# Order of the vector work in a seven-product channel mixer: the fourth sum's two halves moved up, the second sum put behind the first ones

## The chip, the cores and the metric

The kernel runs on one core of a Trainium2 chip. A core has five engines with instruction queues of their own: TensorE (PE, matrix products; its weight loads are shown apart as PEld), VectorE (DVE, elementwise work), ScalarE (ACT, activations, copies and casts), GpSimd (POOL) and SyncE (SP), which here only issues transfers. The engines meet through semaphores alone: an instruction waits in its queue until what it reads has been written and what it overwrites has been read, and everything behind it in the same queue waits too.

The metric is the device time of one launch in microseconds. A difference of about 0.2% (2.7 us) is what a measurement of this kernel can tell from no change.

## The reference

The reference is a two-layer encoder trunk for 512 positions of width 1024, in float32. Each layer has a mixer (layer 0 a recurrent time mixer, layer 1 chunked attention, each beside attention into 256 memory tokens) and then a channel mixer. The change lies in the channel mixer, which is the same in both layers:

```python
def conv_glu(h, w_in, conv_w, conv_b, w_out):
    seq = h.shape[1]
    gate, val = jnp.split(h @ w_in, 2, axis=-1)
    gp = jnp.pad(gate, ((0, 0), (CONV_W - 1, 0), (0, 0)))
    conv = conv_b + sum(conv_w[j] * gp[:, j:j + seq] for j in range(CONV_W))
    return (jax.nn.gelu(conv, approximate=False) * val) @ w_out
```

The hidden width is 2816, that is 22 tiles of 128 gate columns and 128 value columns; the convolution has three taps along the positions. What the mixer returns is added to the residual stream.

## The kernel before

Activations lie transposed in on-chip memory: 128 features on the partitions, 512 positions along the row. Products keep float32 accuracy by splitting both factors into a rounded high half and the rest as a low half, and adding high x high, high x low and low x high. For weights the cast to the high half is done by ACT (`high`, L468) and the subtraction that leaves the low half by DVE (`lower`, L473).

Of the 22 hidden tiles of a layer, tiles 0 to 5 and 21 are computed plainly (`plain`). Tiles 6 to 20 go "by seven": the product of gate and value weights with the activations is cut into 2 x 2 blocks (gate or value columns; first or second half of the input features; first or second half of the positions), and seven block products of sums and differences replace the eight that the plain way needs (the scheme of Strassen and Winograd). Each of these 15 tiles has one call of `Seven.frame`; one call is a frame below. In the profile, layer 0 has its 15 frames from 456 to 611 us and layer 1 from 1033 to 1188 us.

The raw weights of a tile lie in one buffer `raw` with seven slots of 128x512: gate half one (G1), gate half two (G2), value half one (V1), value half two (V2), and the sums S2, S3, S1. The slot of V1 later takes the fourth sum S4. There are two such buffers, so tile j+1 uses the one that tile j-1 has left. Three transfers fill it, issued by SP at L441 (G2 and V2, 512 KB) and L443 (V1, then G1, 256 KB each), as soon as the last reader of the old tile is through.

The sums are DVE's:
- the first ones, `sums` (L455): S3 = G1 + V1 and S1 = V2 + V1 in one instruction of 128x1024;
- the second, `sum2` (L460): S2 = S1 + G1;
- the fourth, `sum4` (L464): S4 = S2 + G2, written where V1 stood.

The casts on ACT then work on neighbouring slots: `high(G1)` casts G1 and S2 together, so it comes after `sum2`.

PE does the seven products of a frame (`prod`, L420 for the two with the weights' high half, L422 for the one with the low half), each with 8 + 4 matmuls of 256 columns, into four accumulators f1 to f4: G1 into f1 (first half), S2 into f2, S3 into f1 (second half), S1 into f3, V2 into f3, G2 into f4, S4 into f4 (second half). A product's low-half matmuls come after its eight high-half ones.

DVE's queue in one frame, before, is in this order (the letters in brackets are used below; "previous" and "next" are the neighbouring tiles):
- [end1] previous tile: add f4 to the gate, L478
- [w31] low half of S3 and S1 of this tile, L473, 128x1024
- [taps] two convolution steps of the previous tile, L485 and L486
- [g] L517, reads f2
- [sums] of the next tile, L455
- [c] L526, reads f1
- [sum2] of the next tile, L460
- [w4] low half of S4 of this tile, L473, 128x512: the last reader of this tile's `raw`
- [end5] previous tile: gate times value, L492
- [gs] low half of G1 and S2 of the next tile, L473, 128x1024
- [sum4] of the next tile, L464
- [v] L537 and [g2] L539, read f3

ACT's queue in one frame: cast of G2 and V2 (L468), copy of f1 (L509), the convolution's first tap for the previous tile (`end2`, L481), the cast of S4 (L468, 128x512), the previous tile's Gelu (`end4`, L489), a negated copy of G2 and V2 of the next tile (`rest`, L450), the cast of G1 and S2 of the next tile, the cast of S3 and S1 of the next tile. Behind `rest`, POOL issues a transfer (L451, 512 KB) that adds the weights once more onto that negated high half, which leaves their low half; this tile of weights is `wlv`.

These instructions are marked to keep the order of the program (`keep`) on their engine. What is not marked, the plain tiles and the splits for the output projection, is put between by a planner.

Of the kernel before, what the change touches and what calls it, by code (L numbers as in the profile page):

```python
# [19 lines left out]
S = 512  # L20
# [92 lines left out]
def trunk_kernel(ctx, tc, A, out):  # L113
# [37 lines left out]
    def ps_f():  # L151
        return banks["F"].tile([P, S], F32, name="psf", tag="psf")
# [8 lines left out]
    def tmp(dt=F32, shape=(P, S)):  # L161
        return banks["tmp"].tile(list(shape), dt, name="tmp", tag="tmp")
# [214 lines left out]
    def ffn(l, hp, U, M, N, new_u, xT, after, last=None):  # L377
# [38 lines left out]
        def prod(ps, w, x):  # L416
            (wh, wl), o = w
            for k in range(4):
                for n in range(2):
                    PE.matmul(ps, wh[:, o + k * P:o + k * P + P], x[k][n], start=k == n == 0, stop=False)  # L420
            for k in range(4):
                PE.matmul(ps, wl[:, o + k * P:o + k * P + P], x[k][0], start=False, stop=k == 3)  # L422
# [3 lines left out]
        def keep(ins):  # L426
            return tc.keep_in_program_order(ins) if pinned[0] else ins
# [3 lines left out]
        S4 = V1  # L431

        class Seven:
# [68 lines left out]
            def frame(self, prev, nxt):  # L502
                if nxt:
                    nxt.load()
                f1, f2, f3, self.f4 = (ps_f() for _ in range(4))
                g, c, v = self.g, self.c, self.v = tmp(), tmp(), tmp()
                prod(f1[:, h1], (self.gs, 0), XN(0, 0))
                hv = self.high(G2)
                keep(SC.copy(g[:, h1], f1[:, h1]))  # L509
                if prev:  # L510
                    prev.end1()
                    prev.end2()
                w31 = self.lower(S3, self.h31)
                if prev:
                    prev.end3()
                prod(f2[:, h1], (self.gs, S), XT(T2))
                keep(V.tensor_tensor(g[:, h2], g[:, h1], f2[:, h1], op=ALU.subtract))  # L517
                h4 = self.high(S4, S)
                if nxt:
                    nxt.sums()  # L520
                if prev:
                    prev.end4()
                if nxt:
                    nxt.rest()
                prod(f1[:, h2], (w31, 0), XT(T3))
                keep(V.tensor_tensor(c[:, h1], f1[:, h2], g[:, h2], op=ALU.subtract))  # L526
                if nxt:
                    nxt.sum2()
                w4 = self.lower(S4, h4, S)
                if prev:  # L530
                    prev.end5()
                prod(f3[:, h2], (w31, S), XT(T1))
                if nxt:
                    nxt.gs = nxt.lower(G1, nxt.high(G1))
                    nxt.sum4()
                prod(f3[:, h1], ((hv, self.low), S), XT(T4))
                keep(V.tensor_tensor(v[:].rearrange("p (a s) -> p a s", a=2), c[:, h1].unsqueeze(1).to_broadcast([P, 2, 256]),  # L537
                                     f3[:].rearrange("p (a s) -> p a s", a=2), op=ALU.add))
                keep(V.tensor_tensor(g[:, h2], g[:, h2], f3[:, h2], op=ALU.subtract))  # L539
                if nxt:  # L540
                    nxt.h31 = nxt.high(S3)
                prod(self.f4[:, h1], ((hv, self.low), 0), XN(4, 0))
                prod(self.f4[:, h2], (w4, 0), XN(4, 1))
# [1092 lines left out]
```

## Time and profile before

| | us |
|---|---|
| median of 3 runs | 1337.94 (1337.45 to 1338.04) |
| the profiled execution, its own time | 1335.9 |
| its span, first to last instruction | 1333.8 |
| PE busy in the span | 1304.6 |
| DVE busy in the span | 941.2 |
| ACT busy in the span | 730.1 |

How to read it: a row of the timeline has the start in us from the span's start, the duration, the engine, the line, the operation, what is written and read, and in brackets the idle time of the engine just before and what ended it. A "q" behind an engine's name is its queue: an instruction that issues a transfer. Instructions of one engine overlap at their ends: a DVE row that lasts 0.68 us may be followed by the next one 0.60 us after its start, so for sums along an engine the distances between starts are used and not the durations. Matmul ends are modelled; the same holds for them.

### The profile page before, as it was taken

What the parts mean: (1) busy time and instruction counts of PE and PEld (TensorE: products, weight loads), DVE (VectorE), ACT (ScalarE), POOL (GpSimd) and SP (SyncE); (2) the same over time, 40 slices, a digit from 0 to 9 for tenths busy, and PEclk for the clock granted to TensorE, in tenths of its full rate; (3) what the DMA queues carried; (4) which work ended last, traced back from release to release, by engine and by line L of the source; (5) the groups of instructions that cost most, each with busy time, mean ns of one, the idle gap of its engine ahead of it and who ended that gap; (6) DMA issues with size and microseconds to landing.
All of it is one profiled execution on the core that took longest, in us unless ns stands there. A gap on an engine that the chain in (4) does not pass through costs nothing. (4 is left out here: it accounts for less than half of the span.)

```text
span 1333.8 us, 25118 instructions
## 1 busy us (share of the span) xinstructions
PE 1304.6 (98%) x10126; PEld 1106.7 (83%) x10126; DVE 941.2 (71%) x1866; ACT 730.1 (55%) x1226; POOL 61.5 (5%) x81
## 2 busy tenths in 40 slices
PE   9999999999999999999999999999999999999996
PEld 7787777777788899998888877786888999998886
DVE  7966866766669899998333675657688899994224
ACT  6666656665445465667232576657455555674221
POOL 0000000000000011110000000000000111100000
PEclk9999999999999999999999999999999999999998
DMA  6365444351232456556333322241324555555332
GB/s 197 109 189 107 90 95 97 86 114 56 97 104 84 119 142 167 143 144 162 90 111 100 124 87 96 87 129 54 111 83 123 134 151 143 149 148 130 101 87 77
DMA packets 76578, 154.05 MB, mean 115 GB/s; under 512 B 20144, under 2 KB 25648, under 8 KB 76464
## 3 DMA queue, kind: packets, MB, share of 16 engines
q1 hardware_dynamic: 64992, 124.94, 29.9%
q0 software_dynamic: 11472, 27.53, 12.5%
q8 instruction: 79, 1.29, 0.4%
q14 instruction: 35, 0.29, 0.1%
HBM read 146.15 MB, written 6.29 MB: 114 GB/s over the span
## 5 line engine op out<-in xcount | busy, mean ns | idle before, releaser
L176 DVE TENSOR_TENSOR wlo<-wraw,whi 128x1024 fp32r<-128x1024 f32 (+1 forms) x117 | 139.1, 1190 | 132.7 <-PE psd L208 113.6
L170 ACT CAST whi<-wraw 128x1024 fp32r<-128x1024 f32 x140 | 143.1, 1024 | 150.1 <-DMA wraw<-in_ffn_out_dram 52.9
L204 PE MATMUL psd<-r1h,whi 128*128 128x512 f32 (+1 forms) x383 | 152.3, 399 | 0.1
L468 ACT CAST whi<-raw 128x1024 fp32r<-128x1024 f32 x120 | 109.0, 938 | 52.0 <-DVE raw L460 26.8
L205 PE MATMUL psd<-r1l,whi 128*128 128x512 f32 x320 | 125.9, 394 | 0.0
L420 PE MATMUL psf<-r2h,whi 128*128 128x256 f32 x420 | 105.5, 284 | 0.0
L420 PE MATMUL psf<-r2l,whi 128*128 128x256 f32 x420 | 105.3, 283 | 0.0
L208 PE MATMUL psd<-r1h,wlo 128*128 128x512 f32 (+1 forms) x383 | 104.2, 397 | 0.0
L473 DVE TENSOR_TENSOR wlo<-raw,whi 128x1024 fp32r<-128x1024 f32 (+1 forms) x90 | 93.9, 1043 | 1.1 <-ACT whi L468 1.1
L204 PEld LDWEIGHTS psd<-r1h,whi 128*128 128x128 f32 x383 | 72.0, 188 | 16.7 <-issue 2.8
L208 PEld LDWEIGHTS psd<-r1h,wlo 128*128 128x128 f32 x383 | 68.7, 188 | 14.6 <-issue 1.4
L420 PEld LDWEIGHTS psf<-r2l,whi 128*128 128x128 f32 x420 | 80.7, 192 | 0.0
L420 PEld LDWEIGHTS psf<-r2h,whi 128*128 128x128 f32 x420 | 80.6, 192 | 0.1
L238 ACT ACTIVATE tmp<-xT 128x512 f32<-128x512 f32 x27 | 17.0, 631 | 101.4 <-DVE xT L599 86.6
L204 PE MATMUL psd<-r2h,whi 128*128 128x512 f32 (+1 forms) x184 | 71.1, 391 | 0.1
L205 PE MATMUL psd<-r2l,whi 128*128 128x512 f32 (+1 forms) x184 | 69.9, 383 | 0.0
L205 PEld LDWEIGHTS psd<-r1l,whi 128*128 128x128 f32 x320 | 60.2, 188 | 10.8 <-issue 0.2
L420 PE MATMUL psf<-r1h,whi 128*128 128x256 f32 x240 | 60.3, 284 | 0.5 <-ACT tmp L509 0.5
L451 POOL DMA_DIRECT2D wlv<-in_ffn_in_dram x30 | 35.8, 1194 | 537.1 <-ACT wlv L450 263.8
L420 PE MATMUL psf<-r1l,whi 128*128 128x256 f32 x240 | 60.1, 283 | 0.0
L422 PE MATMUL psf<-r2h,wlo 128*128 128x256 f32 x300 | 49.0, 286 | 1.1 <-DVE wlo L473 1.0
L455 DVE TENSOR_TENSOR raw<-raw 128x1024 f32<-128x1024 f32 x30 | 36.7, 1222 | 16.0 <-DMA raw<-in_ffn_in_dram 14.9
(478 smaller groups left out, 3378.8 us busy)
## 6 DMA issues: line engine op xcount, KB each, us to landing
raw<-in_ffn_in_dram SPq DMA_DIRECT2D x30, 512.0 KB, 5.9
raw<-in_ffn_in_dram SPq DMA_DIRECT2D x60, 256.0 KB, 6.4
wlv<-in_ffn_in_dram POOLq DMA_DIRECT2D x30, 512.0 KB, 6.0
wraw<-in_ffn_in_dram SPq DMA_DIRECT2D x28, 512.0 KB, 3.5
wraw<-in_ffn_out_dram SPq DMA_DIRECT2D x32, 448.0 KB, 3.5
wraw<-in_wA_dram SPq DMA_DIRECT2D x20, 512.0 KB, 4.1
wraw<-in_w_out_dram SPq DMA_DIRECT2D x16, 512.0 KB, 3.5
wraw<-in_ffn_out_dram SPq DMA_DIRECT2D x16, 512.0 KB, 3.7
```

The source lines that it names most:

```text
L170: SC.copy(hi[:, :n], raw)
L176: V.tensor_tensor(lo[:, :n], raw, hi[:, :n], op=ALU.subtract)
L204: PE.matmul(ps, wh[:, j * P:(j + 1) * P], ah, start=start and n == 0, stop=False)
L205: dense_at[0] = PE.matmul(ps, wh[:, j * P:(j + 1) * P], al, start=False, stop=False)
L208: dense_at[0] = PE.matmul(ps, wl[:, j * P:(j + 1) * P], act(k)[0], start=False, stop=stop and n == len(ks) - 1)
L238: SC.activation(sq[:], src, AF.Square)
L420: PE.matmul(ps, wh[:, o + k * P:o + k * P + P], x[k][n], start=k == n == 0, stop=False)
L422: PE.matmul(ps, wl[:, o + k * P:o + k * P + P], x[k][0], start=False, stop=k == 3)
L451: GP.dma_start(self.low[:].rearrange("p (a s) -> p a s", a=2), self.second, accum_op=ALU.add)
L455: keep(V.tensor_tensor(raw[:, S3:S1 + 1], raw[:, G1:V2 + 1:3], raw[:, V1:V1 + 1].to_broadcast([P, 2, S]), op=ALU.add))
L468: keep(SC.copy(hi[:, :n], self.pair(what) if n > S else self.raw[:, what]))
L473: keep(V.tensor_tensor(lo[:, :n], self.pair(what) if n > S else self.raw[:, what], hi[:, :n], op=ALU.subtract))
```

## The change

In `Seven.frame`, for DVE's queue:
- [w4], the low half of S4, moves from behind [sum2] to a place directly behind the convolution's [taps] and ahead of [g]. Its cast on ACT is now called at the same place in the program; in ACT's own queue it stands where it stood, behind `end2` and ahead of the Gelu.
- [sum2] moves from behind [c] to a place directly behind [sums].

So the order becomes end1, w31, taps, w4, g, sums, sum2, c, end5, gs, sum4, v, g2. Nothing is added or taken away, and no transfer, cast or product is written differently.

```diff
                 if prev:
                     prev.end3()
                 prod(f2[:, h1], (self.gs, S), XT(T2))
+                w4 = self.lower(S4, self.high(S4, S), S)
                 keep(V.tensor_tensor(g[:, h2], g[:, h1], f2[:, h1], op=ALU.subtract))
-                h4 = self.high(S4, S)
                 if nxt:
                     nxt.sums()
+                    nxt.sum2()
                 if prev:
                     prev.end4()
                 if nxt:
                     nxt.rest()
                 prod(f1[:, h2], (w31, 0), XT(T3))
                 keep(V.tensor_tensor(c[:, h1], f1[:, h2], g[:, h2], op=ALU.subtract))
-                if nxt:
-                    nxt.sum2()
-                w4 = self.lower(S4, h4, S)
                 if prev:
                     prev.end5()
                 prod(f3[:, h2], (w31, S), XT(T1))
```

## The prediction

> **What bounds the kernel now.** I read the page's busy times first, then a table of busy time over the two stretches of frames, then PE's timeline at the frames' borders, then who waited for whom, and last DVE's, SP's, POOL's and ACT's timelines of neighbouring frames.
>
> ```profile
> PE 1304.6 (98%) x10126; PEld 1106.7 (83%) x10126; DVE 941.2 (71%) x1866; ACT 730.1 (55%) x1226; POOL 61.5 (5%) x81
> ```
>
> PE has something in flight for 98% of the span, so only what shortens PE's queue or its few waits can move the end. Over the whole span DVE is at 71%; in the frames it is not.
>
> ```profile
> 456.00:601.00 145.00, 143.98 (x1183) 142.39 (x1182) 130.90 (x191) 85.98 (x112) 16.70 (x14) 1.00 0.57 144
> ```
>
> The columns are PE, PEld, DVE, ACT, POOL, granted clock, DMA share and GB/s. DVE is busy 130.90 of 145 us with PE at full clock: two engines run at nearly the same pace here, and a small wait on DVE can reach PE.
>
> ```profile
> 456.38 0.28 PE L420 MATMUL psf<-r2h,whi 128*128 128x256 f32 x1
> ...
> 466.45 0.28 PE L420 MATMUL psf<-r2h,whi 128*128 128x256 f32 x1
> ...
> 476.53 0.28 PE L420 MATMUL psf<-r2h,whi 128*128 128x256 f32 x1
> ...
> 600.54 0.28 PE L420 MATMUL psf<-r2h,whi 128*128 128x256 f32 x1
> ...
> 604.05 0.39 PE L420 MATMUL psf<-r1h,whi 128*128 128x256 f32 x1 [0.47 <-ACT tmp L509]
> ...
> 1033.41 0.28 PE L420 MATMUL psf<-nh,whi 128*128 128x256 f32 x1
> ...
> 1178.09 0.28 PE L420 MATMUL psf<-nh,whi 128*128 128x256 f32 x1
> ```
>
> These are first matmuls of frames. An undisturbed frame lasts 476.53 - 466.45 = 10.08 us: 84 matmuls, 0.12 us apart, 1.44 for a product. The first 14 frames of layer 0 take 600.54 - 456.38 = 144.16 instead of 14 x 10.08 = 141.12, so 3.04 us are lost; those of layer 1 take 1178.09 - 1033.41 = 144.68, 3.56 lost. Together 6.60 us. The last frame of layer 0 also loses about half a microsecond to ACT's copy (the 604.05 row).
>
> ```profile
>   DVE wlo L473: 7.3, 23
> ...
> ACT whi L468 <- DVE raw L460: 26.8, 15, 2.8
> DVE raw L455 <- DMA raw<-in_ffn_in_dram: 14.9, 15, 1.9
> ```
>
> The first row (what PE's psf matmuls idled for, with total and times) says who takes the 6.60 us: PE waits for a low half from DVE. The third says what DVE itself waits for: in 15 of 30 frames [sums] stands still until the next tile's weights land, 14.9 us in all.
>
> ```profile
> 530.48 0.69 DVE L478 TENSOR_TENSOR tmp<-tmp,psf 128x512 f32<-128x512 f32 x1
> 531.08 1.22 DVE L473 TENSOR_TENSOR wlo<-raw,whi 128x1024 fp32r<-128x1024 f32 x1
> 532.22 0.74 DVE L485 SCALAR_TENSOR_TENSOR tmp<-tmp,vec 128x511 f32<-128x511 f32 x1
> 533.00 0.75 DVE L486 SCALAR_TENSOR_TENSOR tmp<-tmp,vec 128x510 f32<-128x510 f32 x1
> 533.66 0.41 DVE L517 TENSOR_TENSOR tmp<-tmp,psf 128x256 f32<-128x256 f32 x1
> 533.99 1.22 DVE L455 TENSOR_TENSOR raw<-raw 128x1024 f32<-128x1024 f32 x1
> 535.13 0.42 DVE L526 TENSOR_TENSOR tmp<-psf,tmp 128x256 f32<-128x256 f32 x1
> 535.46 0.68 DVE L460 TENSOR_TENSOR raw<-raw 128x512 f32<-128x512 f32 x1
> 536.06 0.69 DVE L473 TENSOR_TENSOR wlo<-raw,whi 128x512 fp32r<-128x512 f32 x1
> 536.66 0.69 DVE L492 TENSOR_TENSOR uh<-tmp 128x512 f32<-128x512 f32 x1
> 537.31 1.23 DVE L473 TENSOR_TENSOR wlo<-raw,whi 128x1024 fp32r<-128x1024 f32 x1
> 538.45 0.68 DVE L464 TENSOR_TENSOR raw<-raw 128x512 f32<-128x512 f32 x1
> 539.05 0.68 DVE L537 TENSOR_TENSOR tmp<-tmp,psf 128x512 f32<-128x512 f32 x1
> 539.65 0.41 DVE L539 TENSOR_TENSOR tmp<-tmp,psf 128x256 f32<-128x256 f32 x1
> 540.17 0.69 DVE L478 TENSOR_TENSOR tmp<-tmp,psf 128x512 f32<-128x512 f32 x1
> ...
> 545.61 1.23 DVE L455 TENSOR_TENSOR raw<-raw 128x1024 f32<-128x1024 f32 x1 [1.84 <-DMA raw<-in_ffn_in_dram]
> ```
>
> One frame of DVE's queue without a wait: 540.17 - 530.48 = 9.69 us against PE's 10.08. DVE can make up 0.39 us a frame, and one transfer wait of 1.84 costs nearly five frames of that. So it is late again and again with [w31], and PE stands.
>
> ```profile
> 525.14 1.20 POOL L451 DMA_DIRECT2D wlv<-in_ffn_in_dram  x1 [9.21 <-ACT wlv L450]
> 527.08 0.38 SPq L441 DMA_DIRECT2D raw<-in_ffn_in_dram  x1
> 535.72 1.19 POOL L451 DMA_DIRECT2D wlv<-in_ffn_in_dram  x1 [9.38 <-ACT wlv L450]
> 536.77 0.38 SPq L441 DMA_DIRECT2D raw<-in_ffn_in_dram  x1
> ```
>
> Why the transfer is late: [w4] ends at 536.06 + 0.69 = 536.75 and SP issues the load at 536.77, so [w4] is what frees the buffer. [sums] of the next frame starts 8.84 us later, at 545.61. The load issued at 527.08 was in time for 533.99, so it took at most 6.91. From the start of [sums] to the end of [w4] is 2.76 us (533.99 to 536.75). That closes a ring inside one frame: sums, w4, load, next sums: 2.76 + 0.02 + 8.84 = 11.62 us with the slow load, 9.69 with the fast one, against 10.08.
>
> **The change, part by part.** Nothing is added or removed; the same instructions are counted in a new order.
>
> *w4 behind the taps.* It now precedes [sums] of its own frame, so [sums] and its wait leave the ring. The load for a frame's [sums] goes out behind the [w4] of the frame before. I place the new frame on PE's clock. DVE caught up is held by ACT, as in the frame that starts at 476.53:
>
> ```profile
> 478.44 0.82 ACT L481 ACTIVATE tmp<-tmp,vec 128x512 f32<-128x512 f32 x1
> 479.19 0.62 ACT L468 CAST whi<-raw 128x512 fp32r<-128x512 f32 x1
> ...
> 479.29 0.75 DVE L485 SCALAR_TENSOR_TENSOR tmp<-tmp,vec 128x511 f32<-128x511 f32 x1 [0.30 <-ACT tmp L481]
> ```
>
> The taps start at 479.29 - 476.53 = 2.76 in the frame. From there by the distances above: second tap 3.54, w4 4.20, its end 4.89, the load out at 4.91; g 4.80, sums 5.13. The load has 10.08 + 5.13 - 4.91 = 10.30 us, where the slow one took 8.84. The wait of 14.9 us goes to zero. The cast of S4 ends at 479.81, that is 3.28, so w4 at 4.20 does not wait for it; only in the first frame of a layer, which has no taps, can it, by the cast's 0.62 us, twice, and there DVE is idle anyway. Queued behind w4 are g, sums and c, now 0.60 later (c 1.20); their readers are PE's next use of f2 and f1, one frame on, which I cost at nothing.
>
> *sum2 behind sums.* Two things cost. First, sum2 reads what sums has just written. The dependent taps start 0.78 apart (532.22, 533.00) though the first lasts 0.74; the independent pair behind starts 0.66 apart. So a dependent instruction starts after the end, and sums to sum2 takes 1.22 + 0.03 = 1.25, where sums to c took 1.14: 0.11 more (bounds 0 and 0.11; I take 0.11). [...] Second, the cast of G1 and S2 on ACT starts when sum2 is through, and gs waits for the cast. In the rows this trip is 537.31 - 535.46 = 1.85, covered by w4 and end5. Now c and end5 alone stand between: 0.60 + 0.33 + 0.65 = 1.58, so gs waits 0.27 (bounds 0 and, were nothing covered, 1.17, the trip less sum2's 0.68; 0.27 follows from the rows).
>
> DVE's frame becomes 9.69 + 0.11 + 0.27 = 10.07, just under PE's 10.08, with no transfer wait on top. From the taps at 2.76 the next end1 is 8.33 later, at 1.01 of the next frame; w31 runs 1.61 to 2.83, and PE needs it at 2 x 1.44 + 0.96 = 3.84. So 1.01 us of room stays, the same each frame. gs runs 8.23 to 9.46 and is needed at 10.08 + 0.96 = 11.04.
>
> *Queues passed.* SP's load is only earlier. It now goes out at 4.91 and POOL's wlv transfer some 1.3 us behind it, where SP came 1.05 to 1.94 us behind POOL. wlv is read one frame later, more than 10 us after its issue:
>
> ```profile
> DMA to landing us min/median/max: 5.8/6.0/8.7
> ```
>
> Nothing for that.
>
> *The sum.* PE's 28 frames without waits: -6.60 us. The last frames' copy waits stay as they are (between 0.5 gained and 0.5 lost, as ACT's queue there is filled by the planner). On the profiled time 1335.9 this gives 1329.3; the median of the runs is 2.04 higher, so 1337.94 - 6.6 = 1331.3.
>
> **The rivals.**
>
> *The loads collide (no change).* Now both transfers start in the same microsecond in every frame. The Trainium skill, page "DMA: Bandwidth & Descriptors", section "Issuing engines are not separate DMA queues", says that transfers of all issuers run on the same 16 engines and interleave. The rows bear out that it matters: 6.91 at most with POOL 1.94 us ahead, 8.84 with 1.05. With a load of D us the ring now spans two frames: D + 0.02 + 9.83 from sums to the next w4's end (10.07 - 0.93 + 0.69), so a frame takes (D + 9.85)/2. It binds above D = 10.3; the gain is gone at 28 x (frame - 10.08) - 2 x 1.01 = 6.6, a frame of 10.39, D = 10.9. That gives 1338 us. Against it: nothing seen is near 10.9. Smaller excess leaves a part: D = 10.7 gives a gain of 3.1, so 1334.8.
>
> *The trip over ACT decides (slower).* DVE's frame has only 0.01 us to spare. If gs waits more than 0.27, each 0.1 us is paid 28 times, less the 1.01 us of room per layer. At 0.31 more the gain is gone, at 0.42 the kernel is 0.2% slower; with 0.5 more it is 28 x 0.49 - 2.0 - 6.6 = 5.1 slower, 1343. The place would be ACT's queue, where `rest` stands ahead of the cast.
>
> ```profile
> 533.84 0.63 ACT L489 ACTIVATE tmp<-tmp 128x512 f32<-128x512 f32 x1 [1.32 <-DVE tmp L486]
> 534.38 1.04 ACT L450 ACTIVATE wlv<-raw 128x1024 fp32r<-128x1024 f32 x1
> 536.22 2.00 ACT L468 CAST whi<-raw 128x1024 fp32r<-128x1024 f32 x2 [0.80 <-PE psf L422]
> ```
>
> Gelu and rest end 1.67 us behind the taps (535.42 - 533.75), at 5.96 of the new frame; sum2 ends at 7.06. ACT is 1.1 us early, which speaks against it.
>
> *The load does not leave earlier (no change).* If another reader of raw or SP's queue held it, only the order would differ: 10.07 a frame and waits as before, about 1338 to 1341. The issue 0.02 behind w4 speaks against it.
>
> **How the numbers follow.** Full gain 0.66, part of it 0.12 (both faster), collision or unmoved load 0.12 (within 0.2%), trip over ACT 0.10 (slower). The bound of 0.2% is 2.7 us, about what a measurement can tell. Predicted 1331.3. Low end: the last frames' half microsecond and 0.5 for the spread of the runs, 1330.0; high end takes in the part gains and most of no change, 1336.8.
>
> **What would show it.** Right: no DMA wait ahead of L455, loads issued about 10 us ahead of it, PE's 14 frames at 141.1 us, gs waiting about 0.3 for L468, taps held by L481 in every frame. Wrong: idle ahead of L455, or ahead of gs over 0.6; PE still waiting for L473; sum2 more than 1.3 behind sums.

## The result and the profile after

The changed kernel takes 1329.59 us (median of 6 runs, 1328.76 to 1330.02); the kernel before took 1337.7 in the runs beside it. The ratio is 0.9942, 95% interval 0.9929 to 0.9954. A second set of the same kernel (`after_again` below) gave 1329.55 and 0.9941 (0.9928 to 0.9955). It is faster, as forecast, by more than forecast: 1331.3 was predicted, with 1330.0 as the low end of the range, and the median lies 0.4 us below that end.

The profiled execution took 1329.3 us, span 1327.3. First the rows of PE's timeline at the frames' borders (start, duration, engine, line):

```profile
457.13 0.28 PE L420 MATMUL psf<-r2h,whi 128*128 128x256 f32 x1
...
598.25 0.28 PE L420 MATMUL psf<-r2h,whi 128*128 128x256 f32 x1
...
1030.61 0.28 PE L420 MATMUL psf<-nh,whi 128*128 128x256 f32 x1
...
1171.72 0.28 PE L420 MATMUL psf<-nh,whi 128*128 128x256 f32 x1
```

14 frames of layer 0 take 598.25 - 457.13 = 141.12 us and those of layer 1 take 141.11: 14 x 10.08 = 141.12 in both. Before they took 144.16 and 144.68. PE loses nothing in the frames any more. The view of the tile psf lists what the instructions on it idled for over the whole trace, PE's own and those of ACT and DVE that read it:

```profile
  PE psf L422: 25.5, 30
  PE psf L208: 15.7, 15
```

Both rows are readers on ACT and DVE that wait for a product; before they stood at 24.8 and 15.7 us. The row of low halves from DVE (7.3 us, 23 times) and that of ACT's copy (1.1 us), for which PE idled, are gone. Here is DVE's frame, from end1 to the next end1, and the transfer of the weights on SP's queue:

```profile
538.84 0.69 DVE L478 TENSOR_TENSOR tmp<-tmp,psf 128x512 f32<-128x512 f32 x1
539.45 1.22 DVE L473 TENSOR_TENSOR wlo<-raw,whi 128x1024 fp32r<-128x1024 f32 x1
540.58 0.75 DVE L485 SCALAR_TENSOR_TENSOR tmp<-tmp,vec 128x511 f32<-128x511 f32 x1
541.37 0.75 DVE L486 SCALAR_TENSOR_TENSOR tmp<-tmp,vec 128x510 f32<-128x510 f32 x1
542.03 0.68 DVE L473 TENSOR_TENSOR wlo<-raw,whi 128x512 fp32r<-128x512 f32 x1
542.64 0.41 DVE L518 TENSOR_TENSOR tmp<-tmp,psf 128x256 f32<-128x256 f32 x1
542.97 1.22 DVE L455 TENSOR_TENSOR raw<-raw 128x1024 f32<-128x1024 f32 x1
544.22 0.69 DVE L460 TENSOR_TENSOR raw<-raw 128x512 f32<-128x512 f32 x1
544.83 0.42 DVE L527 TENSOR_TENSOR tmp<-psf,tmp 128x256 f32<-128x256 f32 x1
545.16 0.68 DVE L492 TENSOR_TENSOR uh<-tmp 128x512 f32<-128x512 f32 x1
546.08 1.23 DVE L473 TENSOR_TENSOR wlo<-raw,whi 128x1024 fp32r<-128x1024 f32 x1 [0.23 <-ACT whi L468]
...
548.94 0.69 DVE L478 TENSOR_TENSOR tmp<-tmp,psf 128x512 f32<-128x512 f32 x1
...
553.06 1.22 DVE L455 TENSOR_TENSOR raw<-raw 128x1024 f32<-128x1024 f32 x1
```

```profile
542.75 0.38 SPq L441 DMA_DIRECT2D raw<-in_ffn_in_dram  x1
```

w4 ends at 542.71, the load leaves at 542.75 and the [sums] that need it start at 553.06, 10.31 us later, without a wait; the list of waits no longer has a row in which DVE's L455 waits for a transfer. A frame of DVE's queue lasts 548.94 - 538.84 = 10.10 us. The one new wait is the one ahead of gs, for the cast on ACT: 0.23 us in this frame, and over all frames 11.2 us where it was 1.1 in two waits.

```profile
DVE wlo L473 <- ACT whi L468: 11.2, 30, 1.6
```

The two kinds of transfer have changed places in time: the raw weights now leave first, at 542.75, and wlv at 544.09. The median time from issue to landing is the last number of these rows:

```profile
raw<-in_ffn_in_dram SPq DMA_DIRECT2D x30, 512.0 KB, 3.9
raw<-in_ffn_in_dram SPq DMA_DIRECT2D x60, 256.0 KB, 4.9
wlv<-in_ffn_in_dram POOLq DMA_DIRECT2D x30, 512.0 KB, 7.7
```

Before, it was 5.9 and 6.4 us for the raw weights and 6.0 for wlv. Nobody waits for either now.

### The profile page after: what moved, and what is told of

Same layout as the page of the kernel before. It is cut to its first block, busy times and chain, and to the rows that moved or that the text cites. A ratio compares the mean times of both kernels' runs of the same rounds, so it can differ in the third digit from the quotient of the medians.

```text
span 1327.3 us, 25118 instructions
## 1 busy us (share of the span) xinstructions
PE 1302.2 (98%) x10126; PEld 1107.3 (83%) x10126; DVE 943.1 (71%) x1866; ACT 732.8 (55%) x1226; POOL 61.3 (5%) x81
## 5 line engine op out<-in xcount | busy, mean ns | idle before, releaser
L468 ACT CAST whi<-raw 128x1024 fp32r<-128x1024 f32 x120 | 113.0, 943 | 52.3 <-issue 28.7
L473 DVE TENSOR_TENSOR wlo<-raw,whi 128x1024 fp32r<-128x1024 f32 (+1 forms) x90 | 93.9, 1043 | 11.2 <-ACT whi L468 11.2
L208 PE MATMUL psd<-r2h,wlo 128*128 128x512 f32 (+1 forms) x184 | 47.1, 386 | 0.0
```

The lines of the kernel that those rows point to most:

```text
L208: dense_at[0] = PE.matmul(ps, wl[:, j * P:(j + 1) * P], act(k)[0], start=False, stop=stop and n == len(ks) - 1)
L468: keep(SC.copy(hi[:, :n], self.pair(what) if n > S else self.raw[:, what]))
L473: keep(V.tensor_tensor(lo[:, :n], self.pair(what) if n > S else self.raw[:, what], hi[:, :n], op=ALU.subtract))
```

## The experiments

Two theories stood against each other. *Release*: w4 was the last reader of the raw weights, so its early place lets the next load leave early, and that alone removes the waits. *Order*: what saves time is the new order of DVE's work itself, sum2 and with it ACT's cast coming early. The first four kernels ran on one chip beside 25 runs of the kernel before (median 1336.49, 1334.55 to 1339.16).

**Only w4 moved.**

```diff
+                w4 = self.lower(S4, self.high(S4, S), S)
                 keep(V.tensor_tensor(g[:, h2], g[:, h1], f2[:, h1], op=ALU.subtract))
-                h4 = self.high(S4, S)
...
                 if nxt:
                     nxt.sum2()
-                w4 = self.lower(S4, h4, S)
```

> The kernel before with only w4 (the low half of S4 and the call of its cast) moved up behind the taps; sum2 stays behind c. Theory release (w4 is the last reader of the raw weights, so the next load leaves earlier and sums no longer waits for it): all of the gain, 1329.6 +- 0.7 us, no DMA wait ahead of L455, and w4 leaves its place between sum2 and gs while c now stands ahead of sum2, so only end5 covers the cast: gs waits about 0.5 us, DVE's frame 9.69 + 0.55 = about 10.2, close to PE's. Theory order (sum2 behind sums starts ACT's cast early and that is what saves the time): at most half of the gain, 1333 to 1336 us.

Measured: 1333.65 us, ratio 0.998 (0.9971 to 0.9989): some of the gain, not all. Release had expected all of it, and by its number alone the run would speak for order. The waits say otherwise: no DMA wait stands ahead of L455 any more, but gs waits 0.56 us for the cast, DVE's frame is 10.29 us, above PE's 10.08, and the last frames of a layer run at about that pace. PE's order had also changed in this kernel: from the middle of a layer on, the planner put the low-half matmuls of a product behind the high halves of the next one, which lets PE bear a later w31 (end1 comes as late as 2.84 us in the frame, 2.07 where the order is held). So the run mixes two things, and was repeated with PE's order held:

```diff
-                    PE.matmul(ps, wh[:, o + k * P:o + k * P + P], x[k][n], start=k == n == 0, stop=False)
+                    keep(PE.matmul(ps, wh[:, o + k * P:o + k * P + P], x[k][n], start=k == n == 0, stop=False))
...
-                PE.matmul(ps, wl[:, o + k * P:o + k * P + P], x[k][0], start=False, stop=k == 3)
+                keep(PE.matmul(ps, wl[:, o + k * P:o + k * P + P], x[k][0], start=False, stop=k == 3))
```

> Only w4 moved, as in the first experiment, with PE's matmuls held in the program's order (there the planner had let the low-half matmuls slide behind the next product). The transfer waits are gone, but the cast of G1 and S2 is covered by end5 alone: gs waits 0.56 us and DVE's frame is 10.29. Theory cover (moving w4 uncovers the cast, moving sum2 covers 0.33 us of it again at the price of the dependent pair): end1 drifts 0.2 us a frame from 1.0 to about 1.9, then each frame lasts 10.29: frames 10 x 0.21 x 2 = about 4 us over the changed kernel's, with what follows at the end of a layer 1333 to 1336 us. If the cover does not matter: 1329.6 us.

Measured: 1336.61 us, ratio 1.000 (0.9991 to 1.001), beside 15 runs of before at 1336.82: just above the range expected, 1333 to 1336. With PE's products in the order of the change, w4's move alone gains nothing. Its trace, DVE's queue around the cast and the totals of waits:

```profile
577.22 0.68 DVE L460 TENSOR_TENSOR raw<-raw 128x512 f32<-128x512 f32 x1
577.82 0.68 DVE L492 TENSOR_TENSOR ul<-tmp 128x512 f32<-128x512 f32 x1
579.06 1.23 DVE L473 TENSOR_TENSOR wlo<-raw,whi 128x1024 fp32r<-128x1024 f32 x1 [0.56 <-ACT whi L468]
```

```profile
DVE wlo L473 <- ACT whi L468: 21.1, 30, 1.6
```

From sum2 to gs it is 579.06 - 577.22 = 1.84 us, the trip over ACT, and only end5 stands between. The waits for transfers (14.9 us before) are gone, but 21.1 us of waits for the cast have come in their place. From the seventh frame on a frame takes about 10.29 us (the last one 10.85). From the first frame's first matmul to the last frame's last one, a layer's 15 frames take 153.50 us here and 151.07 in the changed kernel, so the frames lose 4.9 us against that kernel, where about 4 were expected; in this profile 1.8 us more are lost behind the frames and 0.5 ahead of them.

**Only sum2 moved.**

```diff
                 if nxt:
                     nxt.sums()
+                    nxt.sum2()
...
-                if nxt:
-                    nxt.sum2()
                 w4 = self.lower(S4, h4, S)
```

> The kernel before with only sum2 moved up behind sums; w4 stays where it was, now behind c. Theory release: the load leaves no earlier (ring of sums, sum2, c, w4, load: 2.87 us plus the load), DVE's frame is 9.69 + 0.11 = 9.80, so the waits for the load stay and the reserve shrinks from 0.39 to 0.28 us: 28 x 0.11 = 3 us slower than before, 1337 to 1342 us. Theory order: part of the gain, 1333 to 1336 us.

Measured: 1338.19 us, ratio 1.0009 (1.0 to 1.0019): no gain, if anything a little slower, at the lower end of what release expected. The waits for the load stay (the last number of this row of the page, of 15.4 us that DVE idled ahead of [sums]), and PE's frames lose 9.5 us (155.75 + 155.89 - 2 x 151.07).

```profile
L455 DVE TENSOR_TENSOR raw<-raw 128x1024 f32<-128x1024 f32 x30 | 36.7, 1224 | 15.4 <-DMA raw<-in_ffn_in_dram 13.7
```

So with PE's order as it is neither half of the change lowers the time by itself: moving w4 takes the transfer wait away and lays the cast bare; moving sum2 puts 0.33 us of c between sum2 and gs and so covers part of it.

**The release without the order.** S4 goes into the free seventh slot of another buffer, `sp`, and not over V1; then w4 does not read the raw weights, and they are free once w31 is through. DVE's order is that of before.

```diff
-                keep(V.tensor_tensor(raw[:, S4], raw[:, S2], raw[:, G2], op=ALU.add))
+                keep(V.tensor_tensor(sp[:, 6], raw[:, S2], raw[:, G2], op=ALU.add))
```
(`high` and `lower` of S4 read it there.)

> The kernel before, its order untouched, with S4 written into a free slot of another buffer (the seventh of sp) and not over V1. w4 then no longer reads the raw weights, and their last reader is w31 or sum4's partner reads, several us earlier. Theory release: the waits for the load are gone and the time is that of the changed kernel, 1329.6 +- 0.7 us, with DVE's frame at 9.69 us and a caught-up DVE. Theory order: no change, 1337.7 us.

Measured: 1331.43 us (4 runs, 1329.65 to 1332.35), ratio 0.9961 (0.9946 to 0.9976). Its frames take 151.07 us in each layer, to the hundredth what they take in the changed kernel. Its DVE in one frame:

```profile
542.04 1.22 DVE L473 TENSOR_TENSOR wlo<-raw,whi 128x1024 fp32r<-128x1024 f32 x1
543.56 0.75 DVE L485 SCALAR_TENSOR_TENSOR tmp<-tmp,vec 128x511 f32<-128x511 f32 x1 [0.30 <-ACT tmp L481]
...
545.34 1.21 DVE L455 TENSOR_TENSOR raw<-raw 128x1024 f32<-128x1024 f32 x1
```

```profile
543.33 0.38 SPq L441 DMA_DIRECT2D raw<-in_ffn_in_dram  x1
```

The load leaves right behind w31, [sums] does not wait, and DVE is so far ahead that it waits for ACT's first tap. In this profile the first frame starts at 460.2 us, 3.0 us later than in the changed kernel's, and that is nearly all that its span has more (3.2 us); the part on repeats comes back to it. The median lies above the 1329.6 +- 0.7 us expected, but not for the old order's sake: the same kernel with one more instruction a frame (`e6_s4_plus`, below) takes 1329.56 us, with its first frame at 457.2. So the release is enough, and the order of the change is not needed for the gain.

**The order without the release.** The changed kernel, with a copy of one column of S4 on DVE where w4 used to be:

```diff
+                keep(V.tensor_copy(junk[:], self.raw[:, S4, 0:1]))
                 if prev:
                     prev.end5()
                 prod(f3[:, h2], (w31, S), XT(T1))
```

> The changed kernel with one more reader of the raw weights: a 128x1 copy from S4 on DVE where w4 used to stand (behind c), so the order of the change stays and the buffer is freed about as late as before. It costs about 0.06 us of DVE a frame by itself. Theory release: the load leaves late again, the ring is 2.3 us plus 0.02 plus 6.9 to 8.8, and with DVE's frame at 10.1 there is no reserve left to make the waits good: slower than the kernel before, 1339 to 1350 us. Theory order: the gain stays, 1329 to 1332 us.

Measured: 1337.86 us, ratio 1.0015 (1.0006 to 1.0024): the gain is gone, and the kernel is a little slower than before; release had expected 1339 or more.

```profile
546.39 1.23 DVE L456 TENSOR_TENSOR raw<-raw 128x1024 f32<-128x1024 f32 x1 [0.89 <-DMA raw<-in_ffn_in_dram]
...
548.60 0.14 DVE L529 COPY junk<-raw 128x1 f32<-128x1 f32 x1
```

```profile
537.74 0.38 SPq L442 DMA_DIRECT2D raw<-in_ffn_in_dram  x1
548.80 0.38 SPq L442 DMA_DIRECT2D raw<-in_ffn_in_dram  x1
```

The load leaves 0.06 us behind the small copy, and [sums] waits for it again:

```profile
DVE raw L456 <- DMA raw<-in_ffn_in_dram: 7.2, 9, 1.1
```

That is half of the 14.9 us of before, yet the frames lose as much, 7.5 us: gs's waits for the cast (9.3 us) stand beside it, and DVE has next to no time left to make a wait good. One column of one instruction, placed late, costs 8 us. With the run before it this decides for release.

**How much DVE has left.** An addition of 128x256 into a scratch tile, 0.33 us from start to start, is added per frame, with PE's order held (it is the order that the kernel before and the changed one have, so holding it is no second change): behind g2 in the changed kernel, and at the same place in the kernel with S4 elsewhere. These two ran beside 16 runs of before at 1336.88.

```diff
                 keep(V.tensor_tensor(g[:, h2], g[:, h2], f3[:, h2], op=ALU.subtract))
+                keep(V.tensor_tensor(junk[:], xT[:, 0, h1], xT[:, 0, h2], op=ALU.add))
```

> The changed kernel with one more instruction on DVE per frame (an addition of 128x256 into a scratch tile behind g2, 0.33 us from start to start), PE's matmuls held in the program's order. DVE's frame was 10.08 us, so it becomes 10.41, above PE's 10.08. Theory release with a full DVE: the room (end1 from 1.04 to about 1.9 us of the frame) is used up in 3 frames, then each frame costs 0.33 us: about 11 x 0.33 x 2 = 7 us slower than the changed kernel, 1336 to 1337 us. If DVE had reserve: 1329.6 us.

> The kernel before in its order with S4 in the free slot of sp, with the same extra instruction of 0.33 us on DVE and PE's matmuls held in order. DVE's frame 9.69 + 0.33 = 10.02, just under PE's 10.08: nothing is lost against that kernel without the extra instruction, 1329.5 to 1332 us. So the order of before without its transfer waits has 0.39 us of reserve a frame, the changed order none.

Measured: the changed kernel goes to 1335.5 us (ratio 0.9989, 0.998 to 0.9998), the other one stays at 1329.56 (0.994, 0.9925 to 0.9954). Behind g2 the changed order has no room for 0.33 us a frame; the old one with early release has, so at least 0.33 of its 0.39 us is there. Of the first, the size came out otherwise than expected: DVE's frame grew by only about 0.13 us, to 10.23, because the addition filled a gap of about 0.19 us ahead of end1, and the 30 frames lose 2.7 us, not 7. The rest of the profile's loss, 4.5 us, lies behind the frames; PE waits there for the last splits of the hidden tiles, and how much of the loss that is was not separated.

The same addition between end5 and gs, where DVE waits for the cast:

```diff
                 if prev:
                     prev.end5()
+                keep(V.tensor_tensor(junk[:], xT[:, 0, h1], xT[:, 0, h2], op=ALU.add))
                 prod(f3[:, h2], (w31, S), XT(T1))
```

> The changed kernel with the same extra DVE instruction of 0.33 us, but put between end5 and gs, where DVE waits 0.23 us for ACT's cast; PE's matmuls held in order. Theory trip (the way sum2, cast, gs sets DVE's frame there): 0.23 of the 0.33 us cost nothing, the frame grows by 0.10 to 10.18, end1 drifts 0.1 us a frame and reaches 1.9 only in the ninth frame: about 1 us over the changed kernel, 1330 to 1332.5 us. If the trip does not matter, DVE's frame grows by the whole 0.33: as behind g2 or more, 1335 us and over.

Measured: 1333.23 us, ratio 0.9973 (0.9961 to 0.9985), above the expected 1330 to 1332.5. In the frames the expectation holds and more: they take 151.07 us in both layers, and DVE's own frame is about 10.10 us.

```profile
545.24 0.68 DVE L493 TENSOR_TENSOR uh<-tmp 128x512 f32<-128x512 f32 x1
545.84 0.42 DVE L531 TENSOR_TENSOR junk<-xT 128x256 f32<-128x256 f32 x1
546.17 1.22 DVE L474 TENSOR_TENSOR wlo<-raw,whi 128x1024 fp32r<-128x1024 f32 x1
```

From end5 to gs it is 546.17 - 545.24 = 0.93 us with the addition between them, 0.92 in the changed kernel without it: the instruction takes the place of the wait. So the changed order does have this time to spare, but only ahead of gs. What is lost, 3.3 us of the span beside the repeat of the changed kernel below, is lost behind the frames:

```profile
626.72 0.50 PE L205 MATMUL psd<-sl,whi 128*128 128x512 f32 x1 [0.22 <-DVE sl L222]
627.05 0.39 PE L204 MATMUL psd<-uh,whi 128*128 128x512 f32 x1
627.32 0.50 PE L205 MATMUL psd<-sl,whi 128*128 128x512 f32 x1
```

```profile
625.97 4.30 DVE L222 TENSOR_TENSOR sl<-ul,uh 128x512 fp32r<-128x512 f32 x7 [0.69 <-ACT uh L221]
```

The seven splits start at 625.97, in the repeat of the changed kernel at 622.82, and PE then goes at their pace, 627.32 - 626.72 = 0.60 us for two matmuls. The planner arranges ACT's and DVE's work behind the frames otherwise in this kernel; how much of the 3.3 us is that, and how much DVE's small delay, was not separated.

**Repeats.** The changed kernel again, and the kernel before three times more with a profile.

> The changed kernel, unchanged, beside more runs of the kernel before. The frames gave 7.4 us in the profile and nothing else should change: 0.9945 of before with a narrower interval, near 1329.5 us. If the 2.04 us between the profiled execution and the median of before, which the prediction carried over to the changed kernel, belonged to both kernels, the median would be 1331 us.

> The kernel before, unchanged, once more with a profile: how much one execution of it differs from another, and where. If its frames depend on how the transfers fall, the 14 frames of a layer lose another sum than 3.04 and 3.56 us, and a DMA wait ahead of L455 stands in other frames; if the difference lies elsewhere, the frames lose the same and the time up to the first frame (456.4 us) or behind the last one differs. Time 1334.5 to 1339 us, as the runs of before so far.

> The kernel before once more with a profile. Two executions so far lost 7.4 and 8.2 us in the 30 frames and reached the first frame at 456.4 and 460.1 us. If the spread of its runs is the frames', this one loses another sum in them (6 to 10 us) and reaches them near 456.4; if it is the part ahead of the frames, the frames lose about 7.5 to 8 and the first frame starts anywhere from 456 to 460 us.

> The same as the run beside it, a fourth execution: frames lost 6 to 10 us and first frame near 456.4 if the frames make the spread; frames lost 7.5 to 8 us and first frame from 456 to 460 us if the part ahead of them does.

The changed kernel: 1329.55 us (1329.25 to 1330.55), first frame at 457.3, frames 151.07 each. The kernel before, profile by profile (us):

| | first frame starts | 30 frames | over 2 x 151.07 | time |
|---|---|---|---|---|
| first profile | 456.4 | 309.58 | 7.4 | 1335.9 |
| before_again | 460.1 | 310.32 | 8.2 | 1340.27 |
| before_third | 457.8 | 309.10 | 7.0 | 1336.94 |
| before_fourth | 457.1 | 309.49 | 7.4 | 1336.7 |

The frames lose nearly the same in each execution, 7.0 to 8.2 us, though the lost time falls in other frames each time. Of these four profiles' spread the larger part lies ahead of the first frame (3.7 us, beside 1.2 in the frames), where the change does nothing. That does not explain the whole spread: the twelve runs of the changed kernel, with the same work ahead of the frames, lie within 1.8 us, the runs of the kernel before within 5.9 (1333.92 to 1339.82). What else widens it stays open.

## Why the prediction was right in its mechanism and wrong in its range

*The release of the raw weights* came out as worked out: the load leaves at 542.75 - 537.77 = 4.98 us of the frame (predicted 4.91), 0.04 us behind w4, has 10.31 us (10.30), and the waits are gone. In the four profiles of the kernel before, the 28 frames of the sum lose 5.6 to 6.9 us, around the 6.60 of the prediction. The kernel with S4 elsewhere gives the same frames without the new order, and the late copy takes the gain away: shown.

*The dependent pair.* sums to sum2 takes 544.22 - 542.97 = 1.25 us, as predicted from the taps.

*The trip over ACT.* 546.08 - 544.22 = 1.86 us (1.85 predicted), the wait 0.23 (0.27), DVE's frame 10.10 in the rows above (10.07), end1 at 1.07 of the frame (1.01). The room was sized right too: where w4 alone is moved with PE's order held, frames begin to lose when end1 comes at 2.07, with the addition behind g2 at 2.02 (2.02 predicted). But the prediction laid this cost on sum2's move, and there it was wrong: w4's move lays the cast bare (0.56 us of wait by itself) and sum2's move takes part of it back. The forecast sum holds for both together only.

*Who takes the loss.* The prediction read the row of 7.3 us as what PE's matmuls idled for. It adds two rows that overlap in time, the weight loads' and the matmuls':

```profile
who waited for it (us, times):
  PEld psf L422: 5.3, 15
  PE psf L422: 2.0, 8
```

So it names who is late, but its total is no measure of the loss; the 6.60 us, taken from the frames' starts, do not depend on it.

*DVE caught up.* One sign of being right did not come: the taps were to be held by L481 in every frame, and they wait for it four times in all (2.0 us). DVE's frame comes out one or two hundredths above PE's 10.08 and not below it, so end1 moves from 1.04 to 1.11 us over a layer's frames, well inside the room.

*The last frames' copy waits stay.* This is the step that failed. The sum put it at nothing, with 0.5 us either way; the last frames of the two layers lost 0.73 and 0.10 us beyond 10.08 in the first profile, and 1.2 to 1.7 together in the other three, and afterwards nothing. So the frames gained 7.4 us and not 6.60. The last frames lose nothing with S4 elsewhere either, and lose 0.9 and 1.0 with sum2 alone, so the loss goes with DVE's lateness. But in each of these kernels the planner also puts ACT's casts of the last frames in another order than before (in layer 0 the copy of f1 starts 3.10 us into the last frame before, 1.84 in the changed kernel), and which of the two made the loss was not separated.

*The base.* The sum was put on 1337.94, the median of three runs, with the 2.04 us between it and the profiled execution carried over. The 25, 16 and 15 runs of before in the later sets have medians of 1336.49, 1336.88 and 1336.82, about 1.2 below. This is the second term that failed: about 1.2 of the 2.04 us came from which three runs were taken, and not from the kernel. The prediction is 1.75 us too high; 1.2 of that is this term and 0.8 the last frames, and they explain it (2.0) within what single profiles differ by. Against the profiled execution's own time, 1335.9 - 6.6 = 1329.3 is what the changed kernel's profile took, but that is a coincidence: the 0.8 gained in the last frames was hidden by a first frame that started 0.75 us later. The range was too narrow below: 0.5 us for the spread came from three runs, and runs of before reach over 5 us. Its low end was also added up wrongly: 1331.3 less the two half microseconds named is 1330.3, and 1330.0 was written; the measured 1329.59 lies below both.

*The rivals.* The collision did not come: the raw weights land earlier than before and wlv 1.7 us later, read by nobody in that time. The page "DMA: Bandwidth & Descriptors" of the Trainium skill, section "Issuing engines are not separate DMA queues", says that both share the same 16 engines; the landing times bear that out, and the load is not the one that suffers. The prediction put SP 1.05 to 1.94 us behind POOL, from two frames; in the next one it was 2.99 (545.40 and 548.39), and over all frames of before it was 1.05 to 3.04. The trip over ACT as what decides was the nearest one: w4 alone, with PE's order held, is that rival come true, at a gs wait of 0.56.

## What to carry to other kernels

Look for the last reader of a buffer whose transfer is late; moving that one instruction, or giving its data another place, was worth 0.6% here with no work taken away. Before moving an instruction, ask what it covers where it stands: here w4 hid a cast on another engine, and with PE's order held the move paid only because a second one put something else there. And take the base of a forecast from as many runs as there are: three of them can lie together and still be a microsecond from the middle.

## What the runs showed of the hardware that was not expected

An instruction on DVE that reads what the one ahead of it wrote started 0.03 us after that one's end (sums at 542.97, 1.22 long, sum2 at 544.22), and an independent one 0.08 us before it (sums at 533.99, 1.22 long, c at 535.13): 1.25 against 1.14 us behind the same 128x1024 addition.

The transfers show what happens when two meet. With POOL's accumulating transfer issued 1.05 us ahead of SP's weights, [sums] could start only 8.84 us after the weights' issue. With SP's 1.3 us ahead, it is POOL's that grows, from a median of 6.0 us to 7.7. In the kernel with S4 elsewhere SP's are 3.7 us ahead, and neither is held up: medians of 3.8 and 4.1 us for the weights' two kinds of transfer, and 5.9 for POOL's.
